# A fused two-layer diffusion step on one core: the last layer's gate modulation moved from the attention output projection into the feed-forward's input half

## The chip, the cores and the metric

One Trainium2 chip, one of its cores. The metric is the device time of one execution in microseconds (us). A core has TensorE (PE, matmuls; PEld are its weight loads), VectorE (DVE), ScalarE (ACT), GpSimd (POOL) and SyncE (SP, which issues most DMA transfers), each with its own instruction queue; they meet only through semaphores.

## The reference

Two trunk layers over 512 latent tokens and 128 context tokens (640 columns in all), width 1024. Each layer is a mixer (attention) and a SwiGLU feed-forward of inner width 2816, each with its own shift, scale and gate, that come from the conditions `c` and `c_ctx`. Cut to what matters here:

```
def ada_modulation(cond, w_mod, b_mod):
    m = jax.nn.silu(cond) @ w_mod + b_mod
    return jnp.split(m, 6, axis=-1)          # sh1, sc1, g1, sh2, sc2, g2

x = x + g1 * mixer_out                       # output projection of the mixer
h = modulate(rms_norm(x, norm_ffn[l]), sh2, sc2)
x = x + g2 * ((silu(gate) * up) @ w_ffn_out) # gate, up = split(h @ w_ffn_in)
```

The change concerns the last of the six, `g2` of layer 1: 1024 values for each of the two conditions. They are first used where the feed-forward's output is added to `x`.

## The kernel before

Activations lie transposed, in 8 tiles of 128 features x 640 tokens (`T`), worked on in two halves of 320 columns (`HT`). Every f32 product is made of three fp32r products: both operands are split into a high part (a copy on ACT) and a low part (a subtraction on DVE), and `mm3` (L184) multiplies high x high, high x low and low x high. So each weight costs ACT and DVE time as well as PE time.

The layers run one after the other. Within a layer, what the change touches:

- **mixer_out** (L982) is the output projection. It runs over 8 output blocks n; for each it loads the weights (`unit`, L172), multiplies, adds gate x product to the residual x[n] (`residual`, L318, DVE) and adds the squares to a running norm sum (`Norm.add`, L204: a square on ACT, an addition on DVE, tile `oanacc` in layer 0 and `ocnacc` in layer 1). The last three blocks are held back in their second half, and while PE multiplies these, the first half's norm is finished (`Norm.rstd`, L214): a matmul with ones (`oanp`, `ocnp`), then Ln and Exp on ACT.
- **gates_beside** (L1882) is called from layer 1's mixer_out after each block. It loads two of the eight gate rows (`wmG`, 512 KB each) and multiplies those loaded before by the Silu of the two condition rows (`cb`, tile tag "ws" of the feed-forward's pool), a DVE product with an accumulated sum for each row and condition (`junkG`, L1890): 16 products. The two Silu run on ACT at n = 0.
- **ModS** (L256) normalises and modulates x for the feed-forward and forms sums of halves (`add_up`, L305). It needs 16 scratch halves. In layer 0 six of them lie in a wide tile with tag "cb", in layer 1 in three tiles with tag "sg".
- **ffn** (L1079), input half: 22 blocks of the hidden width. Blocks 0 and 1 use eight products per half (`eight`); blocks 2 to 21 are the loop at L1320, where seven products of half the width take the place of eight. In a block PE runs products named by their operands (11, D, E of the block before, N, 21, 22, C). DVE and ACT work in an order written out by hand: `Line` (L1098) makes each DVE instruction follow the one before it, and so for ACT. Weights of block fb + 1 are summed and split during block fb (`Weights`, L1188). The hidden tile of a block is `sg`, its other factor `up`.
- In layer 1 (`paired`) blocks 7 to 18 form six pairs. `split_pair` (L1288) handles the hidden tile of the block before in three stages per block, and turns a pair into seven kinds of tiles (B11, B21, B22, T1 to T4) that go out to DRAM. The first block of a pair has the light share (two low halves, one subtraction), the second the heavy one. A pair's first tile must stay until the second's block is done. `sg` has three buffers of its own in layer 1; in layer 0 it shares the three buffers of tag "t" (`tmp`, L101) with `up`.
- **mod_side** (L1623) is how layer 0's feed-forward computes other modulations beside its work: `start` loads both condition rows into a tile "cb" through SP, `step("load", fb)` issues a row's load in the block before, and `step("fb", fb, dve)` puts the two products (`junk`) into DVE's written order, after the split stage and before `up`. For blocks 5 to 21 of layer 0 it is one row a block. Layer 1 passes a function that does nothing (L1912).
- **ffn**, output half: nine or ten first blocks (`FIRST`) are multiplied whole, the residual is added; then, in layer 1, seven products (`PLAN`, L1499) over the kinds of tiles, fetched from DRAM by `fetch_kind` (L1417). The last three kinds (T4, T1, B22; 18 tiles) go into slots that the first half of the output frees (L1548).

The order of each engine's queue is set by a planner from priorities and dependencies, except where `after` or a `Line` fixes it. Tiles with one tag share its buffers in rotation: a new one waits for the last reader of the oldest.

Of the kernel before, what the change touches and what calls it, by code (L numbers as in the profile page):

```python
# [11 lines left out]
F32 = mybir.dt.float32  # L12
# [37 lines left out]
def body(ctx, tc, xT, vecs, crow, wm0, wm0g, wm1, wA, wNV, wNA, wMK, wMV, wOA, wGQ, wGK, wGV, wOC,  # L50
# [50 lines left out]
    def tmp(name):  # L101
        return tp.tile([P, T], F32, tag="t", bufs=3, name=name)
# [153 lines left out]
    class ModS:  # L256


        def __init__(self, name, x, gsl, ml, sh, pools):
            pool, keep_, paired = pools  # L260

            if paired:
                a = [keep_.tile([P, T], F32, tag="sg", bufs=3, name=f"{name}32a{i}") for i in range(3)]
            else:
                a = [keep_.tile([P, 2 * D], F32, tag="cb", bufs=1, name=name + "32a")]
            d = [pool.tile([P, 1024], F32, tag="wr", bufs=2, name=f"{name}32d{i}") for i in range(2)]
            d += [pool.tile([P, 1024], F32, tag="w4", bufs=2, name=f"{name}32e{i}") for i in range(2)]
            room = [t[:, j * HT:j * HT + HT] for t, n in zip(a + d, ((2, 2, 2) if paired else (6,)) + (3, 3, 3, 1)) for j in range(n)]
            self.left, self.right = room[:KT], room[KT:]
            self.name, self.x, self.gsl, self.ml, self.sh = name, x, gsl, ml, sh  # L270
            self.act = {}
            self.q = [[ring.tile([P, T], F32R, tag=("hh", "hl")[i], name=f"{name}q{k}{i}") for k in range(KT)] for i in range(2)]
            self.sums = {c: [pool.tile([P, T], F32R, tag="sums", bufs=16, name=f"{name}{c}{k}") for k in range(4)]
                         for c in "DCNE"}
# [704 lines left out]
                wh, wl = un(w0)  # L979
                proj(pss[u][c], wh[0], wh[1], hh, hl, [k], *HALF[c], first=first and j == 0, last=last and j == n - 1, w0=wl)  # L980

    def mixer_out(wsrc, os_, order, xin, ml, name, nxt, pre, beside=None):  # L982

        nrm = Norm(name + "n", D)
        oh, ol = [o[0] for o in os_], [o[1] for o in os_]
        x = []
        ks = [(k, k) for k in order]
        if True:
            def wunit(n):
                get = lazy(lambda: unit(wsrc[n], 1024, f"{name}w{n}", lo="g" if n % 2 else "v"))  # L990
                return lambda w0: (get(), w0)

            def evac(n, c, ps):
                if c == 0:
                    x.append(xin(n))
                residual(x[n], x[n], ps, ml, G1, n, c)
                nrm.add(x[n], c)

            def half(ps, un, c, ks, first=True, last=True):
                two_halves([ps], [un], ks, oh, ol, c, first=first, last=last)  # L1000

            held = []
            units = [wunit(n) for n in range(KT)]
            for n in range(KT):
                un = units[n]
                if n < 2:
                    ps = pair(f"{name}{n}")
                    for c in range(2):
                        half(ps, un, c, ks[:-1], last=False)
                    held.append((ps, un))  # L1010
                    if n == 1:
                        for i, (ps, un) in enumerate(held):
                            for c in range(2):
                                half(ps, un, c, ks[-1:], first=False)
                                evac(i, c, ps[c])
                        held = []
                elif n < 5:
                    ps = pair(f"{name}{n}")
                    for c in range(2):
                        half(ps, un, c, ks)  # L1020
                        evac(n, c, ps[c])
                else:
                    ps = pair(f"{name}{n}") if n < 7 else [bank(f"{name}{n}{c}") for c in range(2)]
                    half(ps, un, 0, ks)
                    evac(n, 0, ps[0])
                    held.append((n, ps, un))
                if beside is not None:
                    if 0 < n < KT - 1:
                        units[n + 1](0)
                    beside(n, nrm.last)  # L1030
            pre()
            for j in range(KT - 2):
                for n, ps, un in held:
                    half(ps, un, 1, ks[j:j + 1], first=j == 0, last=False)
                if j >= 1:
                    nxt(x, nrm, 0, (j - 1,))
            for i, (n, ps, un) in enumerate(held):
                half(ps, un, 1, ks[-2:], first=False)
                evac(n, 1, ps[1])
                nxt(x, nrm, 0, (5 + i,))  # L1040
        return x, lambda: nxt(x, nrm, 1, range(KT))

    def next_mod(name, gsl, ml, sh, sums=None):

        box = {}

        def nxt(x, nrm, c, ks):
            if 0 in ks:
                nrm.rstd(c)
                if c == 0:  # L1050
                    box["m"] = Mod(name, x, gsl, ml, sh) if sums is None else ModS(name, x, gsl, ml, sh, sums)
            for k in ks:
                box["m"].make(c, nrm.rs, k)
        return box, nxt
# [24 lines left out]
    def ffn(l, x, pend, hm, nxt, side, opened):  # L1079
# [204 lines left out]
            dve(V.tensor_tensor, out, a, b, ALU.subtract)  # L1284

        over = {}

        def split_pair(jb, sg, stage):  # L1288
            i, j = PAIR_OF[jb]
# [30 lines left out]
        for fb in range(FEW, FB):  # L1320
# [2 lines left out]
            n = Weights(fb + 1) if fb < FB - 1 else None  # L1323
            b5 = bank(f"fd{l}_{fb}")
            up = tmp(f"up{l}_{fb}")
            sg = fk.tile([P, T], F32, tag="sg", bufs=3, name=f"sg{l}_{fb}") if paired else tmp(f"sg{l}_{fb}")
            both = paired and job and job[0] in PAIR_OF
            p5, u1, g2 = [utile(f"{c}{l}_{fb}") for c in ("p5", "u1", "g2")]
            if n:
# [68 lines left out]
        dve(V.tensor_tensor, jsg, jup, jsg, ALU.mult)  # L1398
        hidden(jb, jsg)
        fs.close()  # L1400

        fo = ph.enter_context(tc.tile_pool(name=f"fo{l}", bufs=1, reuse_waits="tile"))

# [5 lines left out]
        for i, fb in enumerate(FIRST[STAY:]):  # L1409
            if i < 6:  # L1410
                again(fb, [ring.tile([P, T], F32R, tag="hh" if i < 4 else "hl", name=f"hr{l}_{fb}{c}") for c in "hl"])
            else:
                again(fb, [fo.tile([P, T], F32R, tag="hd", bufs=26, name=f"hr{l}_{fb}{c}") for c in "hl"])
        later = [(c, i) for c in ("T2", "B11", "T3", "B21") for i in range(len(PAIRS))] if paired else list(SECOND)
        kinds = {}

        def fetch_kind(c, i, pool, tag):  # L1417
# [4 lines left out]
        def some(n):  # L1422
            for _ in range(min(2 * n if paired else n, len(later))):
                fb = later.pop(0)
                if paired:
                    fetch_kind(*fb, fo, "hd")
                    continue
                again(fb, [fo.tile([P, T], F32R, tag="hd", bufs=2 * len(SECOND), name=f"hr{l}_{fb}{c}") for c in "hl"])
# [48 lines left out]
        for i, (n, j0, m) in enumerate(jobs):  # L1477
# [5 lines left out]
            if j0 + m == len(FIRST):  # L1483
# [3 lines left out]
                    some(2)  # L1487
                step("n", n)
        some(len(later))

        exp_tables(last)
        nrm = Norm(f"fn{l}", D)
# [5 lines left out]
        if paired:  # L1498
# [48 lines left out]
                weights(j)  # L1547
            spots = [("hl", 4), ("hh", 8), ("hl", 4), ("fo", 2)]  # L1548
            spots = [c for c, n in spots for _ in range(n)]
            for c, i in [(c, i) for c in ("T4", "T1", "B22") for i in range(len(PAIRS))]:  # L1550
                tag = spots.pop(0)
                fetch_kind(c, i, *((fo, "hd") if tag == "fo" else (ring, tag)))
            for p in range(4):
# [112 lines left out]
        return xk  # L1666

    op = ffn_open(0)
    box, nxt = next_mod("h01", gs[0][1], mods[0], SH2, (op[5], op[1], False))
    x, pend = mixer_out(wOA, oMs + oNs, [4, 5, 6, 7, 0, 1, 2, 3], x_again, mods[0], "oa", nxt, op[-1])  # L1670
    box2, nxt = next_mod("h10", gs[1][0], mods[1], SH1)
    side = mod_side([(0, wm0g, G2)] + [(1, wm1[j:j + 8], j) for j in (SH1, SC1, G1, SH2, SC2)],
# [200 lines left out]

    open_y(y=4)
    op = ffn_open(1)
    box, nxt = next_mod("h11", gs[1][1], mods[1], SH2, (op[5], op[1], True))
    cb = [op[5].tile([P, D], F32, tag="ws", bufs=2, name=f"cb{c}") for c in range(2)]
    for c in range(2):
        nc.scalar.dma_start(cb[c], bass.AP(tensor=crow.tensor, offset=crow.offset + D * c, ap=[[0, P], [1, D]]))
    gates = []  # L1880

    def gates_beside(n, done):  # L1882
        if n == 0:
            for c in range(2):
                S.activation(cb[c], cb[c], AF.Silu)
        while gates:
            i, raw = gates.pop(0)
            for c in range(2):
                junk = op[1].tile([P, D], mybir.dt.bfloat16, tag="junk", bufs=1, name=f"junkG{i}{c}")
                after(done, lambda: V.scalar_tensor_tensor(junk, raw, 1.0, cb[c], ALU.mult, ALU.mult,  # L1890
                                                           accum_out=mods[1][:, G2 + i, c:c + 1]))
        if n < 4:
            for i in (2 * n, 2 * n + 1):
                raw = op[5].tile([P, D], F32, tag="wr", bufs=2, name=f"wmG{i}")
                nc.sync.dma_start(raw, wm1[G2 + i])
                gates.append((i, raw))
        elif n == 4:
            m = mods[1][:, G2:G2 + 8, :]
            V.tensor_tensor(m, m, bc2(bmod(1, G2, 8)), ALU.add)

    x, pend = mixer_out(wOC, oGs, list(range(8)), lambda n, x=x: x[n], mods[1], "oc", nxt, op[-1], gates_beside)

    def final(x, nrm, c, ks):
        c0, c1 = HALF[c]
# [4 lines left out]
            (nc.sync if k % 2 else nc.scalar).dma_start(yT[:, k, c0:c1], x[k][:, c0:c1])  # L1909
        return last  # L1910

    x, pend = ffn(1, x, pend, box["m"], final, lambda fk: lambda *a: None, op)  # L1912
    pend()


# [154 lines left out]
```

## Time and profile before

| what | value |
|---|---|
| median of 3 runs | 1523.57 us (1522.32 to 1525.17) |
| profiled execution | 1523.39 us, its span 1521.6 us |
| PE, DVE, ACT, POOL busy | 1459.4, 1192.5, 767.3, 223.5 us |
| moved by DMA | 226.89 MB, mean 149 GB/s |
| layer 1's 16 gate products (junkG), 1039 to 1074 us | 23.5 us of DVE |
| one block of the input half, either layer | 12.34 us |

How to read it: busy times are of one execution, in us. A group of instructions is shown as line, engine, operation, output<-input, shapes, count | busy us, mean ns | idle time before it and who ended it. In an order of time, the first two columns are start and duration in us, and "[0.67 <-PE fd L62]" is the time that the engine sat idle before the instruction and what released it. In the view of windows the columns are: length in us, then busy time and number of instructions of PE, PEld, DVE, ACT and POOL, the granted TensorE clock (1.00 is full), the busy share of the DMA engines and GB/s. The names of layer 0 begin with oa, h01; those of layer 1 with oc, h11; fg, fu, fd are banks of the feed-forward's input half, fo those of its output half.

### The profile page before, as it was taken

The numbers are of one execution on the slowest core, as the hardware profiler recorded it, in microseconds if no ns is written. First come the engines' busy times: TensorE is split into PE (matmuls) and PEld (weight loads), VectorE is DVE, ScalarE is ACT, GpSimd is POOL, SyncE is SP. The second block draws the span as 40 slices with busy tenths as digits, with TensorE's granted clock in tenths as the row PEclk, the third lists the DMA queues.
The fourth block names the chain that finished last, engine by engine and source line by source line (L and its number), as shares of the span: only waits on it lengthen the run. The fifth ranks groups of instructions, "written<-read, shape, count | busy, mean of one in ns | idle before, by whom it ended". The sixth has DMA issues, their size and how long they took to land.

```text
span 1521.6 us, 25799 instructions
## 1 busy us (share of the span) xinstructions
PE 1459.4 (96%) x9856; PEld 1404.0 (92%) x9856; DVE 1192.5 (78%) x2234; ACT 767.3 (50%) x1506; POOL 223.5 (15%) x295
## 2 busy tenths in 40 slices
PE   5999989989999999999999999999899999999996
PEld 4888878879999999999999889989899999999996
DVE  5646687885899999967998787778898889854486
ACT  5535586773755444441124556663665555542242
POOL 0225544522000000000002433222000000000000
PEclk9999999999999999999999999999999999999998
DMA  9324540005155555569763210014235445458531
GB/s 371 115 94 152 186 143 34 29 15 181 55 177 177 179 184 188 176 228 342 258 213 114 91 42 29 29 66 143 98 136 163 161 161 192 163 200 312 189 112 69
DMA packets 79579, 226.89 MB, mean 149 GB/s; under 512 B 8816, under 2 KB 14208, under 8 KB 79328
## 3 DMA queue, kind: packets, MB, share of 16 engines
q1 hardware_dynamic: 77120, 220.84, 42.8%
q10 hardware_dynamic: 1920, 3.47, 0.7%
q8 instruction: 77, 1.26, 0.3%
q0 software_dynamic: 416, 0.93, 0.2%
q14 instruction: 46, 0.38, 0.1%
HBM read 190.86 MB, written 34.36 MB: 148 GB/s over the span
## 4 chain that ended last, share of the span: by engine, by line
PE 77%; DVE 13%; ACT 4%; DMA 4%; issue 2%; POOL 0%; DVEq 0%; SPq 0%; ACTq 0%; POOLq 0%
PE fg L62 19%; PE fd L62 9%; PE fo L62 7%; PE fu L62 5%; PE gq L62 2%; PE nk L62 2%; PE fo_2b L62 1%; PE nq L62 1%; PE go L62 1%; DVE junkG L1890 1%; DMA mraw<-in_wm 1%; PE fo_2a L62 1%; PE ms L62 1%; PE gs L62 1%; PE mod L62 1%
## 5 line engine op out<-in xcount | busy, mean ns | idle before, releaser
L1104 ACT ACTIVATE sg<-g 128x320 f32<-128x320 f32 x40 | 18.9, 472 | 132.2 <-DVE g L1104 132.2
L1638 DVE SCALAR_TENSOR_TENSOR junk<-wm,cb 128x1024 bf16<-128x1024 f32 x62 | 75.7, 1221 | 6.4 <-DMA wm<-in_wm 5.7
L62 PE MATMUL gq<-h10h,wgq 128*128 128x320 f32 x256 | 66.4, 319 | 0.4 <-DVE gb L1821 0.3
L251 POOL TENSOR_SCALAR h10h<-h10t,gs,mods 128x320 fp32r<-128x320 f32 x4 | 3.5, 887 | 429.4 <-DVE h10t L245 427.7
L1104 DVE TENSOR_TENSOR wY<-s,wY 128x1024 fp32r<-128x1024 f32 x40 | 48.8, 1220 | 1.1 <-ACT wY L1104 1.1
L1104 DVE TENSOR_TENSOR wZ<-s,wZ 128x1024 fp32r<-128x1024 f32 x40 | 48.8, 1219 | 0.0
L62 PEld LDWEIGHTS gq<-h10h,wgq 128*128 128x128 f32 x256 | 45.3, 190 | 1.6 <-PE gtp L66 0.8
L1104 ACT ACTIVATE wZ<-s 128x1024 fp32r<-128x1024 f32 x40 | 42.4, 1060 | 1.1 <-DVE s L1104 1.0
L1104 ACT ACTIVATE wY<-s 128x1024 fp32r<-128x1024 f32 x40 | 42.0, 1049 | 0.0
L1104 DVE SCALAR_TENSOR_TENSOR junk<-wm,cb 128x1024 bf16<-128x1024 f32 x34 | 41.5, 1220 | 0.6
L1822 ACT ACTIVATE gp<-gs,gb,rq 128x640 f32<-128x640 f32 (+1 forms) x40 | 31.9, 797 | 19.5 <-DVE gb L1821 15.4
L1104 DVE TENSOR_TENSOR sg<-up,sg 128x640 f32<-128x640 f32 (+1 forms) x40 | 31.4, 786 | 12.2 <-ACT sg L1104 12.2
L62 PE MATMUL gq<-h10l,wgq 128*128 128x320 f32 x128 | 39.8, 311 | 0.0
L62 PE MATMUL fg<-h11E,wW 128*128 128x320 f32 x240 | 38.7, 310 | 0.4 <-DVE g L1104 0.4
L62 PE MATMUL fd<-h11q,wZ 128*128 128x320 f32 x240 | 38.6, 310 | 0.2 <-ACT p L1104 0.2
L62 PE MATMUL fg<-h11N,wZ 128*128 128x320 f32 x240 | 38.7, 309 | 0.0
L62 PE MATMUL fg<-h11q,wX 128*128 128x320 f32 x240 | 38.6, 309 | 0.0
L62 PE MATMUL fg<-h01q,wX 128*128 128x320 f32 x240 | 38.6, 309 | 0.0
L62 PE MATMUL fg<-h01N,wZ 128*128 128x320 f32 x240 | 38.6, 309 | 0.0
L62 PE MATMUL fu<-h11q,wX 128*128 128x320 f32 x240 | 38.6, 309 | 0.0
L62 PE MATMUL fu<-h01q,wX 128*128 128x320 f32 x240 | 38.6, 309 | 0.0
L62 PE MATMUL fg<-h01E,wW 128*128 128x320 f32 x240 | 38.6, 310 | 0.0
(3187 smaller groups left out, 5295.3 us busy)
## 6 DMA issues: line engine op xcount, KB each, us to landing
wm<-in_wm SPq DMA_DIRECT2D x40, 512.0 KB, 4.0
mraw<-in_wm SPq DMA_DIRECT2D x24, 512.0 KB, 3.6
mraw<-in_wm SPq DMA_DIRECT2D x8, 1024.0 KB, 15.3
hr_T<-sp_T SPq DMA_DIRECT2D x24, 320.0 KB, 6.1
hr_B<-sp_B SPq DMA_DIRECT2D x18, 320.0 KB, 6.7
wm<-in_wm0g SPq DMA_DIRECT2D x8, 512.0 KB, 3.4
wmG<-in_wm SPq DMA_DIRECT2D x8, 512.0 KB, 4.2
x<-in_xT SPq DMA_DIRECT2D x8, 320.0 KB, 5.4
```

The lines of the kernel that those rows point to most:

```text
L62: cls.last = nc.tensor.matmul(*a, **k)
L251: G.tensor_scalar(h[:, c0:c1], t, self.gsl[:, k, 0:1], self.ml[:, self.sh + k, 0:1], ALU.mult, ALU.add)
L1104: self.last = after(self.last, lambda: op(*a, **k))
L1638: def step(kind, at, line=lambda op, *a, **k: op(*a, **k)):
L1822: S.activation(dst, src, AF.Exp, bias=nb, scale=rq[:, j:j + 1], accum_out=ll[:, j:j + 1])
L1890: after(done, lambda: V.scalar_tensor_tensor(junk, raw, 1.0, cb[c], ALU.mult, ALU.mult, accum_out=mods[1][:, G2 + i, c:c + 1]))
```

## The change

gates_beside, its condition rows and its call go, and so does mixer_out's hook for it. Layer 1's feed-forward gets a mod_side of its own: one gate row in each of blocks 5, 6, 8, 10, 12, 14, 16 and 18. That needs the tile "cb" (8 KB of each partition) in a pool that had the three "sg" tiles, so these go: a pair's first hidden tile is `lead`, a ninth tile of the residual's tag and so in the place of x[0]. x[0] is written to DRAM before the loop and read back into `lead` after it. All other `sg` of layer 1 are `tmp` tiles, as in layer 0. ModS uses the "cb" tile for its scratch halves in both layers. After the gates, the "cb" tile holds three of the six T4 tiles (`more`), fetched ahead of the other kinds.

```diff
         def __init__(self, name, x, gsl, ml, sh, pools):
-            pool, keep_, paired = pools
-            if paired:
-                a = [keep_.tile([P, T], F32, tag="sg", bufs=3, name=f"{name}32a{i}") for i in range(3)]
-            else:
-                a = [keep_.tile([P, 2 * D], F32, tag="cb", bufs=1, name=name + "32a")]
+            pool, keep_ = pools
+            a = keep_.tile([P, 2 * D], F32, tag="cb", bufs=1, name=name + "32a")
...
-    def mixer_out(wsrc, os_, order, xin, ml, name, nxt, pre, beside=None):
+    def mixer_out(wsrc, os_, order, xin, ml, name, nxt, pre):
...
-                if beside is not None:
-                    if 0 < n < KT - 1:
-                        units[n + 1](0)
-                    beside(n, nrm.last)
...
         over = {}
+        if paired:
+            x0 = dr.tile([P, T], F32, name=f"x0_{l}")
+            nc.sync.dma_start(x0, x[0])
+            lead = ring.tile([P, T], F32, tag="x", name=f"lead{l}")
...
-            sg = fk.tile([P, T], F32, tag="sg", bufs=3, name=f"sg{l}_{fb}") if paired else tmp(f"sg{l}_{fb}")
+            sg = lead if paired and PAIR_OF.get(fb, (0, 1))[1] == 0 else tmp(f"sg{l}_{fb}")
...
         fs.close()
+        if paired:
+            nc.sync.dma_start(lead, x0)
+            x = [lead] + x[1:]
...
+        if paired:
+            wide_ = fk.tile([P, 2 * D], F32R, tag="cb", bufs=1, name=f"more{l}")
+            more = [wide_[:, j * T:(j + 1) * T] for j in range(3)]
...
         some(len(later))
+        if paired:
+            for i, t in enumerate(more):
+                nc.sync.dma_start(f(t), solo["T4", i])
+                kinds["T4", i] = t
...
-            for c, i in [(c, i) for c in ("T4", "T1", "B22") for i in range(len(PAIRS))]:
+            for c, i in [(c, i) for c in ("T4", "T1", "B22") for i in range(len(PAIRS))][len(more):]:
...
-    box, nxt = next_mod("h11", gs[1][1], mods[1], SH2, (op[5], op[1], True))
-    cb = [op[5].tile([P, D], F32, tag="ws", bufs=2, name=f"cb{c}") for c in range(2)]
-    for c in range(2):
-        nc.scalar.dma_start(cb[c], bass.AP(tensor=crow.tensor, offset=crow.offset + D * c, ap=[[0, P], [1, D]]))
-    gates = []
-    def gates_beside(n, done):
...
-    x, pend = mixer_out(wOC, oGs, list(range(8)), lambda n, x=x: x[n], mods[1], "oc", nxt, op[-1], gates_beside)
+    box, nxt = next_mod("h11", gs[1][1], mods[1], SH2, (op[5], op[1]))
+    x, pend = mixer_out(wOC, oGs, list(range(8)), lambda n, x=x: x[n], mods[1], "oc", nxt, op[-1])
...
-    x, pend = ffn(1, x, pend, box["m"], final, lambda fk: lambda *a: None, op)
+    side = mod_side([(1, wm1[G2:], G2)], lambda kind, i: int(kind == "fb" and i in (5, 6, 8, 10, 12, 14, 16, 18)))
+    x, pend = ffn(1, x, pend, box["m"], final, side, op)
```

More of the change, by code (lines that the diff above doesn't have):

```diff
@@ L259, in __init__ @@
         def __init__(self, name, x, gsl, ml, sh, pools):
-            pool, keep_, paired = pools
-            if paired:
-                a = [keep_.tile([P, T], F32, tag="sg", bufs=3, name=f"{name}32a{i}") for i in range(3)]
-            else:
-                a = [keep_.tile([P, 2 * D], F32, tag="cb", bufs=1, name=name + "32a")]
+            pool, keep_ = pools
+            a = keep_.tile([P, 2 * D], F32, tag="cb", bufs=1, name=name + "32a")
             d = [pool.tile([P, 1024], F32, tag="wr", bufs=2, name=f"{name}32d{i}") for i in range(2)]
             d += [pool.tile([P, 1024], F32, tag="w4", bufs=2, name=f"{name}32e{i}") for i in range(2)]
-            room = [t[:, j * HT:j * HT + HT] for t, n in zip(a + d, ((2, 2, 2) if paired else (6,)) + (3, 3, 3, 1)) for j in range(n)]
+            room = [t[:, j * HT:j * HT + HT] for t, n in zip([a] + d, (6, 3, 3, 3, 1)) for j in range(n)]
             self.left, self.right = room[:KT], room[KT:]
@@ L1668, in body @@
     op = ffn_open(0)
-    box, nxt = next_mod("h01", gs[0][1], mods[0], SH2, (op[5], op[1], False))
+    box, nxt = next_mod("h01", gs[0][1], mods[0], SH2, (op[5], op[1]))
     x, pend = mixer_out(wOA, oMs + oNs, [4, 5, 6, 7, 0, 1, 2, 3], x_again, mods[0], "oa", nxt, op[-1])
@@ L1875, in body @@
     op = ffn_open(1)
-    box, nxt = next_mod("h11", gs[1][1], mods[1], SH2, (op[5], op[1], True))
-    cb = [op[5].tile([P, D], F32, tag="ws", bufs=2, name=f"cb{c}") for c in range(2)]
-    for c in range(2):
-        nc.scalar.dma_start(cb[c], bass.AP(tensor=crow.tensor, offset=crow.offset + D * c, ap=[[0, P], [1, D]]))
-    gates = []
-    def gates_beside(n, done):
[L1883 to L1899, printed above, removed]
-    x, pend = mixer_out(wOC, oGs, list(range(8)), lambda n, x=x: x[n], mods[1], "oc", nxt, op[-1], gates_beside)
+    box, nxt = next_mod("h11", gs[1][1], mods[1], SH2, (op[5], op[1]))
+    x, pend = mixer_out(wOC, oGs, list(range(8)), lambda n, x=x: x[n], mods[1], "oc", nxt, op[-1])
     def final(x, nrm, c, ks):
```

## The prediction, made before the changed kernel ran

> **What bounds the kernel now.** I read the page first: TensorE (PE) is busy 96% of the span, and the chain that ended last is mostly PE lines. Of what the change moves, one VectorE (DVE) line shows in it, junkG, with 1%, about 15 us.
>
> ```profile
> span 1521.6 us, 25799 instructions
> ...
> PE 1459.4 (96%) x9856; PEld 1404.0 (92%) x9856; DVE 1192.5 (78%) x2234; ACT 767.3 (50%) x1506; POOL 223.5 (15%) x295
> ...
> PE fg L62 19%; PE fd L62 9%; PE fo L62 7%; PE fu L62 5%; PE gq L62 2%; PE nk L62 2%; PE fo_2b L62 1%; PE nq L62 1%; PE go L62 1%; DVE junkG L1890 1%; DMA mraw<-in_wm 1%; PE fo_2a L62 1%; PE ms L62 1%; PE gs L62 1%; PE mod L62 1%
> ```
>
> So a saving counts only where PE waits. The waits of PE, next, show two that this change can touch: the layer 1 norm sum (ocnp) waits 6.2 us for DVE, and one product of the feed-forward's output half (fo_1b) waits 0.8 us for a weight copy. Layer 0's norm sum (oanp), computed by the same function without gates beside it, waits 0.6.
>
> ```profile
> PE ocnp L62 <- DVE ocnacc L211: 6.2, 2, 6.0
> ...
> PE fo_1b L62 <- ACT wo_1S L1534: 0.8, 1, 0.8
> PE oanp L62 <- DVE oanacc L211: 0.6, 1, 0.6
> ```
>
> The kernel holds its own control experiment. Layer 0 runs mixer_out, ModS and ffn with no gates in the projection and with its modulation in the feed-forward's input half, as layer 1 will. I compare the two from the chain in order of time (start, us, what), between marks that both have: the second projection product and the first fg product of the loop's second block.
>
> ```profile
> 342.57 3.08 PE oa0b L62 x21
> ...
> 447.13 3.52 PE fg L62 x24
> ...
> 1023.85 3.08 PE oc0b L62 x21
> ...
> 1137.61 3.52 PE fg L62 x24
> ```
>
> The windows between these marks (us; busy time and instructions of PE, PEld, DVE, ACT, POOL; granted clock; DMA) hold the same 705 matmuls:
>
> ```profile
> 342.57:447.13 104.56, 103.96 (x705) 103.27 (x705) 78.38 (x152) 54.33 (x104) 13.32 (x8) 1.00 0.40 135
> 1023.85:1137.61 113.76, 106.64 (x705) 104.67 (x705) 96.14 (x177) 62.33 (x111) 13.64 (x8) 0.97 0.38 129
> ...
> 1076.60:1080.10 3.50, 3.49 (x11) 3.10 (x12) 0.00 (x0) 2.19 (x4) 0.00 (x0) 0.50 0.78 272
> ```
>
> Layer 1 takes 113.76 - 104.56 = 9.20 us longer. Of that, 113.76 - 106.64 = 7.12 against 0.60 is idle PE (6.5 us more), and 106.64 - 103.96 = 2.7 us is slower PE: after the long wait the granted clock stands at 0.50 for 3.5 us.
>
> **Part 1: the gates leave the projection.** Removed there are 16 products on DVE and their accumulator reads, eight 512 KB loads on SP, two Silu on ACT and two loads of the condition rows.
>
> ```profile
> L1890 DVE SCALAR_TENSOR_TENSOR junkG<-wmG,cb 128x1024 bf16<-128x1024 f32 x16 | 23.5, 1471 | 0.1
> ...
> 1078.08 0.53 ACT L218 ACTIVATE ocnrs<-ocnp,eps 128x320 f32<-128x320 f32 x1 [1.28 <-PE ocnp L62]
> 1078.63 1.28 ACT L219 ACT_TABLE_LOAD   x1
> 1079.92 0.47 ACT L219 ACTIVATE ocnrs<-ocnrs 128x320 f32<-128x320 f32 x1
> ...
> L218 ACT ACT_TABLE_LOAD x2 | 2.6, 1283 | 0.0
> L219 ACT ACT_TABLE_LOAD x2 | 2.6, 1283 | 0.0
> ```
>
> 23.5 us of DVE goes, where DVE sits in front of the residuals and norm sums on which ocnp waits. The early Silu also replaced the table that holds Ln and Exp together: each half's rstd then reloads twice, 4 x 1.28 us, and the Silu itself once. What is late next without them is what layer 0 shows: its ocnp twin waits 0.6 us, nothing else in that stretch of PE waits visibly. So the stage gives 9.20 us. Ends: all of PE's idle gone would be 9.8; if only the wait of 6.2 went and the rest stayed behind another cause, 6.2. I take 9.20, since it is a measured difference over equal work.
>
> At most three of the four stand on a chain (after the first, Ln still waits 1.28 us for PE): 3 x 1.28 = 3.8 us, part of the 9.20 and not beside it. The Trainium skill (ScalarE: Activation LUTs, section What ACT_TABLE_LOAD costs) puts a switch at 1.28 us for the load and 1.38 for a drain, 2.66 together; by that these would be 8.0 us, and the part of the stage that they could explain 4.2 us larger. The trace does not show the drain here: Ln ends at 1078.61, the load starts at 1078.63, and Exp starts 0.01 us after it.
>
> **Part 2: the gates enter the input half.** PE is busy without a gap there in both layers, 12.33 to 12.34 us a block (rows below), so the added work is free as long as DVE keeps up. Price of a pair of products, from layer 0's loop: from 544.42 to the next operation at 546.83, 2.41 us; eight pairs are 19.3 us. They go to blocks 5, 6, 8, 10, ... 18: where pairs are split, only to the even blocks, which carry the light share of the split. The DVE column of four windows of a block each, cut at DVE's own block start (odd, even), and a layer 0 block with its gate pair:
>
> ```profile
> 1225.96:1238.29 12.33, 12.33 (x86) 12.33 (x85) 11.94 (x21) 7.46 (x14) 0.00 (x0) 1.00 0.43 150
> 1238.29:1250.63 12.34, 12.34 (x86) 12.34 (x85) 10.20 (x16) 6.27 (x11) 0.00 (x0) 1.00 0.62 209
> ...
> 533.48:545.81 12.33, 12.33 (x86) 12.33 (x85) 11.99 (x20) 6.06 (x10) 0.00 (x0) 1.00 0.58 188
> ...
> L1104 DVE SCALAR_TENSOR_TENSOR junk<-wm,cb 128x1024 bf16<-128x1024 f32 x34 | 41.5, 1220 | 0.6
> ...
> 544.42 1.22 DVE L1104 SCALAR_TENSOR_TENSOR junk<-wm,cb 128x1024 bf16<-128x1024 f32 x1
> ...
> 546.83 0.48 DVE L1104 TENSOR_TENSOR up<-fd,u 128x320 f32<-128x320 f32 x1
> ```
>
> An even block becomes 10.20 + 2.41 = 12.61, over the 12.33; with the odd one, 12.61 + 11.94 = 24.55 of 24.67. It fits by 0.12. Place by place: in an even block the last split half ends near 1247.8, and DVE then idles 0.67 and 1.26 us. The row of PE is that of the next block's E product.
>
> ```profile
> 1247.37 0.49 DVE L1104 TENSOR_TENSOR hd_2l<-sg,hd_2l 128x320 fp32r<-128x320 f32 x1
> 1248.54 0.49 DVE L1104 TENSOR_TENSOR up<-fd,u 128x320 f32<-128x320 f32 x1 [0.67 <-PE fd L62]
> 1250.29 0.49 DVE L1104 TENSOR_TENSOR g<-fg,p 128x320 f32<-128x320 f32 x1 [1.26 <-PE fg L62]
> ...
> 1253.62 1.92 PE L62 MATMUL fg<-h11E,wW 128*128 128x320 f32 x12
> ...
> 1262.61 0.49 DVE L1104 TENSOR_TENSOR g<-fg,p 128x320 f32<-128x320 f32 x1 [0.29 <-PE fg L62]
> ```
>
> The gate pair runs 1247.8 to 1250.2, up follows to 1250.6, and g starts 0.3 us late. Behind the gate on DVE stand up, g and the next block's weight sums; behind g, ACT's Silu. PE needs g's bank again at 1253.62 for the E product, 1253.62 - 1250.78 = 2.8 us after g has read it now, so 0.3 is covered; the odd block's own 0.29 of idle gives it back. Weight halves have more room: those of a block are written in the block before. Cost taken: nothing; ends: 0 and the whole 19.3 if DVE's idle could not be filled. I stay at zero: layer 0 does it at 11.99 of 12.33 without a wait of PE.
>
> **Part 3: SP, spill and buffers.** Three transfers of 320 KB are new in kind: x[0] out before the loop, back after it, and the lead tile waits for the first at the end of block 7. A 320 KB load takes 5.4 us, and block 7 comes some 60 us later. On the way back the reload waits for the last split's reads, at 1335.8; queued behind it on SP is the first hidden block, which leaves only at 1349.23 now; x[0] is used at 1377.95. Cover 13 and 42 us, cost zero; with that cover gone it would be the transfer, 5.4. The second halves of pairs take the shared temporaries, as every block of layer 0 does, so I charge nothing. The condition rows now load through SP, where they wait for ModS's room, with spills queued behind: in layer 0 the first of these leaves at 429.75, 17.4 us before the mark 447.13, in layer 1 now at 1121.53, 16.1 before 1137.61, so nothing is later for it.
>
> ```profile
> x<-in_xT SPq DMA_DIRECT2D x8, 320.0 KB, 5.4
> ...
> 1335.32 0.48 DVE L1104 TENSOR_TENSOR hd_0l<-sg,hd_0l 128x320 fp32r<-128x320 f32 x1
> ...
> 1349.23 0.32 SPq L1406 DMA_DIRECT2D hr_0h<-sp_0h  x1
> ...
> 1377.95 0.55 DVE L322 SCALAR_TENSOR_TENSOR xr<-fo_0a,mods,xr 128x320 f32<-128x320 f32 x1 [0.64 <-PE fo_0a L62]
> ...
> 429.75 0.33 SPq L1138 DMA_DIRECT2D sp_0h<-hd_0h  x1
> ...
> 1121.53 0.33 SPq L1138 DMA_DIRECT2D sp_0h<-hd_0h  x1
> ```
>
> **Part 4: three T4 tiles early.** The old gate-row tile takes them before the rest. Today all of these loads fill SP when the first output half ends:
>
> ```profile
> 1428.20 7.83 SPq L1419 DMA_DIRECT2D hr_T<-sp_T  x12
> 1436.53 4.97 SPq L1419 DMA_DIRECT2D hr_B<-sp_B  x6
> 1442.65 0.33 SPq L1506 DMA_DIRECT2D wo_3A22r<-in_wFO  x1
> ```
>
> 18 loads take 1442.65 - 1428.20 = 14.45 us, 0.80 each; three fewer bring the weight behind them 2.4 us forward, and PE waited 0.83 for what is made of it. Gain 0.83; ends 0 (they collide with other weights) and 0.83.
>
> **The sum.** The profiled execution took 1523.39 us (span 1521.6); the median is 0.18 above. 1523.39 - 9.20 - 0.83 = 1513.36; against the median, 1513.5.
>
> **Rivals.** (1) DVE becomes the bound. The Trainium skill (Perfetto Trace Analysis, Identifying the Most-Contended Engine) calls VectorE's occupancy a fair measure of how near it is to its limit and would have the most contended engine improved. The mechanism by rows: 24.55 of 24.67 is 99.5%; if the idle places of DVE are not where the gates come, they lengthen the eight blocks by 2.41 each, 19.3 less the 2.8 that the bank's lead hides once, and the end is 1513.5 + 16.5 = 1530.0: slower. It turns from gain to loss when a pair of blocks is over by (10.0 + 2.8) / 6 = 2.1 us, a product of 2.3 us instead of 1.22. Against it: POOL, beside which junkG averaged 1.47 us, is idle in this half, and layer 0's 34 products average 1.22. Layer 0 does not bear the rule out at 97%; 99.5% no run shows yet. Chance 0.04. (2) Something other than the gates holds layer 1's norm sum, and only the 6.2 of the wait returns, or DVE's lag costs PE a few us: 1523.57 - 6.2 - 0.83 = 1516.5, up to 1520. Against it: equal matmuls and the same code in layer 0. Chance 0.16. (3) The freed time comes back as another wait altogether (a spill, the reload of x[0]), within 0.2%: 0.03. That T4's early loads go out no earlier costs 0.83, 1514.3, inside the forecast, which has 0.77.
>
> **Numbers.** About 0.2%, 3 us, can be told from no change. Faster by more: 0.77 + 0.16 = 0.93; same 0.03; slower 0.04. The low end is the 9.8 and 0.83 off the median, 1512.9, less 1.2 for the spread of the runs below it (1522.32), 1511.7; the high end is rival 2 with as much more, 1517.7.
>
> **What would show it.** Right: no wait of ocnp above 1 us, granted clock 1.00 throughout the projection, two table loads fewer per rstd, the marks 104.6 us apart, blocks still 12.34 us with DVE near 12.6 and 11.9, no fo_1b wait. Wrong: PE waiting for DVE or ACT inside the loop, blocks longer where gates are, or products well over 1.22 us.

## The result, and the profile after

The changed kernel takes 1512.2 us (median of 6 runs, 1509.52 to 1518.67) against 1523.53 (6 runs, 1521.34 to 1525.17): a ratio of 0.9931 with a 95% interval of 0.9911 to 0.9951, so 7.5 to 13.6 us faster. By the medians it is 11.3 us; the forecast was 1513.5, or 10.0 us. The profiled execution took 1513.06 us; the sum, made against the profiled time, had said 1513.36. That the two lie 0.3 us apart is in part luck, since executions of the changed kernel spread over 9 us; the stages below are the better test.

The page of the kernel after: span, busy times, and the chain that ended last by engine and by line. No line of the gates is left in it, and PE's share of the chain has grown to 84%.

```profile
span 1511.3 us, 25796 instructions
...
PE 1455.6 (96%) x9856; PEld 1401.0 (93%) x9856; DVE 1191.1 (79%) x2234; ACT 760.1 (50%) x1501; POOL 224.6 (15%) x295
...
PE 84%; DVE 8%; ACT 4%; DMA 2%; issue 2%; POOL 0%; DVEq 0%; SPq 0%; ACTq 0%; POOLq 0%
PE fg L62 20%; PE fd L62 9%; PE fo L62 7%; PE fu L62 6%; PE gq L62 2%; PE nq L62 2%; PE nk L62 2%; PE fo_2b L62 1%; PE fo_0b L62 1%; DMA mraw<-in_wm 1%; PE go L62 1%; PE fo_2a L62 1%; PE fo_0a L62 1%; PE mod L62 1%; PE ms L62 1%
```

The waits of PE, after. The two layers' norm sums now wait alike, and fo_1b, which stood between them in the list before, waits no more:

```profile
PE ocnp L62 <- DVE ocnacc L211: 0.6, 1, 0.6
PE oanp L62 <- DVE oanacc L211: 0.6, 1, 0.6
```

The windows, after: layer 1 between the two marks of the prediction, then the rest of the program cut at the loop's end and at three places of the output half (the columns are those of the prediction's windows).

```profile
1023.89:1128.45 104.56, 103.96 (x706) 103.27 (x705) 77.85 (x144) 53.84 (x104) 13.60 (x8) 1.00 0.30 103
...
1128.45:1343.14 214.69, 214.69 (x1467) 214.61 (x1466) 204.34 (x317) 117.99 (x209) 0.00 (x0) 1.00 0.56 189
1343.14:1415.38 72.24, 72.24 (x495) 72.13 (x494) 27.24 (x46) 16.94 (x26) 0.00 (x0) 1.00 0.71 245
1415.38:1461.10 45.72, 45.72 (x314) 45.72 (x314) 34.08 (x57) 18.33 (x29) 0.00 (x0) 1.00 0.52 182
```

The same cuts in the kernel before:

```profile
1137.61:1352.30 214.69, 214.69 (x1466) 214.62 (x1466) 186.70 (x284) 116.59 (x207) 0.00 (x0) 1.00 0.49 163
1352.30:1424.54 72.24, 72.24 (x494) 72.13 (x494) 27.70 (x47) 17.31 (x27) 0.00 (x0) 1.00 0.71 245
1424.54:1470.26 45.72, 44.89 (x306) 44.63 (x306) 33.21 (x53) 17.54 (x27) 0.00 (x0) 1.00 0.57 199
```

The reader sees where the time went. Between the marks, 113.76 us became 104.56, with the same matmuls and full clock. In the loop, DVE rose from 186.7 to 204.3 us and PE did not notice: 214.69 us both times. In the output half's middle, PE gets through 314 matmuls in 45.72 us instead of 306. Nothing was given back elsewhere.

### The profile page after: what moved, and what is told of

Read it like the earlier page. It is cut to its first block, busy times and chain, and to the rows that moved or that the text cites. A ratio compares the mean times of both kernels' runs of the same rounds, so it can differ in the third digit from the quotient of the medians.

```text
span 1511.3 us, 25796 instructions
## 1 busy us (share of the span) xinstructions
PE 1455.6 (96%) x9856; PEld 1401.0 (93%) x9856; DVE 1191.1 (79%) x2234; ACT 760.1 (50%) x1501; POOL 224.6 (15%) x295
## 3 DMA queue, kind: packets, MB, share of 16 engines
q8 instruction: 77, 1.26, 0.3%
## 4 chain that ended last, share of the span: by engine, by line
PE 84%; DVE 8%; ACT 4%; DMA 2%; issue 2%; POOL 0%; DVEq 0%; SPq 0%; ACTq 0%; POOLq 0%
PE fg L62 20%; PE fd L62 9%; PE fo L62 7%; PE fu L62 6%; PE gq L62 2%; PE nq L62 2%; PE nk L62 2%; PE fo_2b L62 1%; PE fo_0b L62 1%; DMA mraw<-in_wm 1%; PE go L62 1%; PE fo_2a L62 1%; PE fo_0a L62 1%; PE mod L62 1%; PE ms L62 1%
## 5 line engine op out<-in xcount | busy, mean ns | idle before, releaser
L1645 DVE SCALAR_TENSOR_TENSOR junk<-wm,cb 128x1024 bf16<-128x1024 f32 x62 | 75.6, 1219 | 7.1 <-DMA wm<-in_wm 6.6
L1097 DVE SCALAR_TENSOR_TENSOR junk<-wm,cb 128x1024 bf16<-128x1024 f32 x50 | 61.0, 1220 | 0.8
L62 PE MATMUL fd<-h01q,wZ 128*128 128x320 f32 x240 | 38.5, 309 | 0.0
L62 PE MATMUL fg<-h11C,wY 128*128 128x320 f32 x240 | 38.5, 309 | 0.0
```

Source lines behind the costliest of these rows:

```text
L62: cls.last = nc.tensor.matmul(*a, **k)
L1097: self.last = after(self.last, lambda: op(*a, **k))
L1645: def step(kind, at, line=lambda op, *a, **k: op(*a, **k)):
```

## The experiments

Times are medians, and each ratio is against runs of the kernel before that were taken beside them. For the stages I use the marks of the trace. Between the two marks, the changed kernel took 104.56 us and the five kernels below that leave this stage as it is 104.57 to 105.1, so differences under 0.6 us there say nothing.

**Which part of the projection cost what.** Two cuts of the kernel before, each alone and both together.

```diff
-                S.activation(cb[c], cb[c], AF.Silu)
+                S.activation(cb[c], cb[c], AF.Copy)
```

> The kernel before, with the Silu of the two condition rows in the projection replaced by a plain copy (the gates then come from the conditions without Silu); no table is switched there, and the 16 products stay. Theory (the products on VectorE hold the norm sum): the wait of ocnp stays near 6 us, the stretch between the marks falls from 113.76 by 0 to 1.5 us, so 1522 to 1523.5 us. Rival (the table loads on the chain are the price): the stretch falls by about 3.8 us or more, to 1519.7 us or less.

Measured: 1521.48 us, ratio 1.0000 (0.9991 to 1.0009). The wait stayed, and the stretch fell by 0.81 us to 112.95:

```profile
PE ocnp L62 <- DVE ocnacc L211: 5.9, 1, 5.9
...
1021.70:1134.65 112.95, 106.72 (x705) 105.30 (x705) 96.87 (x177) 55.84 (x106) 13.87 (x8) 0.97 0.39 130
```

```diff
-                after(done, lambda: V.scalar_tensor_tensor(junk, raw, 1.0, cb[c], ALU.mult, ALU.mult,
-                                                           accum_out=mods[1][:, G2 + i, c:c + 1]))
+                after(done, lambda: V.tensor_tensor(mods[1][:, G2 + i, c:c + 1], raw[:, :1], cb[c][:, :1], ALU.mult))
```

> The kernel before, with each of the 16 gate products cut to one column (the gates are then not the sums); loads, Silu and table switches stay. Theory: 23.5 us of VectorE go, the wait of ocnp falls below 1 us plus at most one table load, the clock stays at 1.00, the stretch falls by 7.5 to 9.2 us to 104.6 to 106.3, the time to 1514.3 to 1516 us. Rival (table loads): the stretch falls by 5.4 us or less, the time stays above 1518 us.

Measured: 1516.3 us, ratio 0.9965 (0.9954 to 0.9977). The wait of ocnp falls from 6.2 to 1.6 us and the clock is full, but the stretch, cut at 705 matmuls, is 106.96: down by 6.80, not by 7.5 to 9.2. My number was missed on the low side; the rival's limit of 5.4 was passed. The first 45.32 us are as in layer 0 with 310 matmuls, and what is missing is missing behind them: 380 matmuls in 59.24 us, against 396 with both cuts.

```profile
PE ocnp L62 <- DVE ocnacc L211: 1.6, 2, 1.3
...
1026.29:1071.61 45.32, 45.32 (x310) 45.06 (x308) 26.04 (x51) 17.32 (x26) 9.70 (x4) 1.00 0.57 198
1071.61:1130.85 59.24, 56.72 (x380) 55.77 (x380) 53.63 (x110) 43.44 (x82) 3.00 (x4) 1.00 0.29 93
...
1026.29:1133.25 106.96, 104.44 (x705) 103.22 (x704) 80.27 (x161) 62.53 (x110) 12.70 (x8) 1.00 0.40 137
```

Both edits together:

> The kernel before with both cuts: one-column products and a copy for the Silu (gates not computed as the reference does); only the loads stay. Both theories: the stretch is 104.6 us, as in layer 0, and the time 1523.5 - 9.2 = 1514.3 us; the fo_1b wait of 0.8 us stays. If the loads on SyncE had a part in it, the stretch stays above 105.5 us.

Measured: 1513.9 us, ratio 0.9948 (0.9933 to 0.9963), stretch 104.58. The row loads on SP and the hook that orders the weight loads, which both stay in this kernel, had no part in it.

```profile
1024.18:1069.50 45.32, 45.32 (x310) 45.32 (x310) 25.08 (x51) 15.80 (x24) 9.72 (x4) 1.00 0.62 209
1069.50:1128.74 59.24, 58.64 (x396) 57.95 (x395) 54.06 (x110) 40.15 (x82) 3.00 (x4) 1.00 0.27 88
...
1024.18:1128.76 104.58, 103.98 (x705) 103.29 (x705) 79.14 (x161) 55.97 (x106) 12.73 (x8) 1.00 0.42 140
```

So of 9.18 us, the products are worth 6.80 if they go first and 8.37 if they go last, and the Silu with its table switches 2.38 if it goes last but only 0.81 if it goes first. As long as the products delay the norm, most of the reloading hides behind that delay. The 0.81 is hardly above the scatter of the marks, and the run times cannot tell it from nothing; the other three prices stand clear of that scatter.

**What the gates cost where they are now.** The products in layer 1's input half, cut to one column:

```diff
+                        if len(todo) == 1:
+                            line(V.tensor_tensor, mods[l][:, j0 + i, c:c + 1], raw[:, :1], cb[:, c, :1], ALU.mult)
+                            continue
                         junk = fp.tile([P, D], mybir.dt.bfloat16, tag="junk", ...)
```

> The changed kernel, with the 16 products in layer 1's input half cut to one column (gates not the sums); rows are still loaded. Theory (VectorE fills idle time there): VectorE falls by about 18 us, the loop's blocks stay at 12.34 us, the time is the changed kernel's within 0.3 us. Rival (VectorE at 99.5% costs PE a little): 1 to 3 us faster than the changed kernel.

Measured: 1511.34 us, ratio 0.9939 (0.9923 to 0.9956), which is the changed kernel's within the intervals; and the loop is exactly as long, while DVE fell by 16.4 us.

```profile
1125.98:1340.67 214.69, 214.69 (x1467) 214.61 (x1466) 187.95 (x301) 118.18 (x209) 0.00 (x0) 1.00 0.56 189
```

**Where free ends.** Each product made twice, so four in a gate block:

```diff
+                      for again in range(1 + (len(todo) == 1)):
...
                         line(V.scalar_tensor_tensor, junk, raw, 1.0, cb[:, c, :], ALU.mult, ALU.mult, ...)
```

> The changed kernel, with each of the 16 products of layer 1's input half made twice (same result): 2.41 us more on VectorE in each gate block. A pair of blocks then needs 24.55 + 2.41 = 26.96 us of VectorE against 24.67. Theory (VectorE runs behind until g is 2.8 us late and then holds PE at the E product): loss of 1.3 us in block 6, 0.9 in block 8, 2.3 in each of 10 to 18: 13.6 us, so about 1526 us, with PE waiting for VectorE's g before the product with wW. Rival A (full price): 19.3 us, 1531.5 us. Rival B (only the weights' lead of 8 us counts): 8.4 us, 1520.6 us.

Measured: 1529.63 us, ratio 1.0049 (1.0032 to 1.0067), 17.4 us above the changed kernel's median. The loop alone, cut at the same marks, takes 231.53 us, 16.84 more. The place is the one expected: PE waits seven times, each time before the product with wW and for g. The size is not; it lies between the theory's 13.6 and the full price of 19.3. The sum of the waits, and five of the seven E products in PE's order of time (what lies between them is left out):

```profile
PE fg L62 <- DVE g L1097: 9.8, 7, 2.1
...
1177.16 2.02 PE L62 MATMUL fg<-h11E,wW 128*128 128x320 f32 x12 [1.26 <-DVE g L1097]
...
1202.82 2.02 PE L62 MATMUL fg<-h11E,wW 128*128 128x320 f32 x12 [0.65 <-DVE g L1097]
...
1229.88 3.38 PE L62 MATMUL fg<-h11E,wW 128*128 128x320 f32 x12 [2.12 <-DVE g L1097]
...
1284.15 3.10 PE L62 MATMUL fg<-h11E,wW 128*128 128x320 f32 x12 [2.12 <-DVE g L1097]
...
1338.51 2.88 PE L62 MATMUL fg<-h11E,wW 128*128 128x320 f32 x12 [2.10 <-DVE g L1097]
```

From 1229.88 to 1284.15 lie two pairs, 27.13 us each and not 26.96: DVE is busy in 53.34 of these 54.27 us, and short gaps between its instructions make up the rest. That is 0.17 a pair more than forecast, 1.0 in all. And wherever the wait was 2.1 us, the 12 matmuls behind it took 2.9 to 3.4 us instead of 2.0. The windows of the same kernel around one such wait, granted clock before the last two columns:

```profile
1227.76:1229.88 2.12, 0.00 (x1) 0.00 (x0) 2.09 (x5) 0.02 (x1) 0.00 (x0) 1.00 0.00 0
1229.88:1231.40 1.52, 1.51 (x6) 1.52 (x7) 1.49 (x3) 1.52 (x3) 0.00 (x0) 0.58 0.90 218
1231.40:1233.07 1.67, 1.67 (x9) 1.67 (x7) 1.64 (x3) 1.67 (x3) 0.00 (x0) 0.50 0.32 125
```

In the middle of the loop PE has to wait for DVE anyhow, so a slow stretch there only takes the place of waiting. The last one comes in the last gate block, and nothing makes up for it: E and the product after it take 5.17 us instead of the 3.64 behind the wait at 1311.35, so 1.5 us are lost. Whether the room before E is really 2.8 us, this run alone leaves open. A run with half the overload, three products in a gate block, helps to tell:

```diff
+                      for again in range(1 + (len(todo) == 1 and c == 0)):
```

> The changed kernel, with one of the two products of a gate block made twice (three products, same result): 1.26 us more in each gate block, half the overload of the run with four. A pair then needs about 25.9 us of VectorE against 24.67. Theory (the room before the E product is used up first, then each pair is held by what it is over): blocks 5 and 6 run 1.7 us behind, block 7 takes that back, blocks 8 and 10 use up the 2.8 us, and 12 to 18 lose about 1.2 each: 4.8 us in the loop, the waits of PE under 1.5 us and the granted clock at 1.00 all through. Rival A (there is no room, every pair loses all of it, as the run with four seemed to): 7 us or more. Rival B (the loss of the run with four was its clock): under 3 us.

Measured: 1516.25 us, ratio 0.9963 (0.9950 to 0.9975). The loop's 1466 matmuls take 219.63 us instead of 214.69, so 4.9 us, as the theory said; the waits are four, in the last four gate blocks, none above 0.93 us, at full clock.

```profile
PE fg L62 <- DVE g L1097: 3.1, 4, 0.9
...
1126.87:1346.50 219.63, 216.50 (x1466) 214.66 (x1466) 212.63 (x333) 115.98 (x209) 0.00 (x0) 1.00 0.57 187
```

Rivals A and B are out: the room exists, is used up first, and from then on each pair loses about what it is over. But the agreement on 4.8 us is in part luck, as the order of time shows. In the gate blocks where PE waits, in this run and in the run with four, PE's queue has the 12 matmuls of fu ahead of E, where the changed kernel goes from D straight to E. The last gate block, of the changed kernel and then of the run with three:

```profile
1316.60 1.92 PE L62 MATMUL fd<-h11D,wY 128*128 128x320 f32 x12
1318.35 1.92 PE L62 MATMUL fg<-h11E,wW 128*128 128x320 f32 x12
```

```profile
1320.46 1.92 PE L62 MATMUL fu<-h11q,wX 128*128 128x320 f32 x12
1323.31 2.03 PE L62 MATMUL fg<-h11E,wW 128*128 128x320 f32 x12 [0.93 <-DVE g L1097]
```

So PE has about 1.76 us more to do before it needs g (12 matmuls of 214.69 / 1466 us), and the room is 2.83 + 1.76 = 4.59 us instead of 2.8. On the other side DVE falls further behind than the theory had it: block 7 does not take all of the delay back, its g is still 1.82 us late. The last gate block's g in the kernel before, in the run with three and in the run with four:

```profile
1324.17 0.49 DVE L1104 TENSOR_TENSOR g<-fg,p 128x320 f32<-128x320 f32 x1 [1.26 <-PE fg L62]
```

```profile
1322.77 0.48 DVE L1097 TENSOR_TENSOR g<-fg,p 128x320 f32<-128x320 f32 x1
```

```profile
1337.97 0.48 DVE L1097 TENSOR_TENSOR g<-fg,p 128x320 f32<-128x320 f32 x1
```

Counted from each kernel's second mark, g comes 9.34 us later with three products and 19.77 us later with four. Less the room of 4.59 this gives 4.75 us, of 4.94 measured, and 15.18 us, which with the 1.5 us of the last slow stretch is 16.7 of the 16.84 measured. That accounts for both runs to within 0.2 us: the price is DVE's delay at the last gate block, less the room, plus the clock. The theory had two terms wrong, room and delay, by about 1.8 us each, and with three products they cancelled.

**Does the place between the light sums matter?** The gates in the heavy blocks:

```diff
-int(kind == "fb" and i in (5, 6, 8, 10, 12, 14, 16, 18))
+int(kind == "fb" and i in (5, 6, 9, 11, 13, 15, 17, 19))
```

> The changed kernel, with the six gates of the pairs in the blocks with the heavy share of the split (9, 11, ... 19) instead of the light ones. VectorE needs 11.94 + 2.41 = 14.35 us in such a block and 10.20 in the next; the sum of a pair is the same. Theory (2.8 us of room before the E product): g is up to 2.1 us late, PE does not wait, same time as the changed kernel within 0.3 us. Rival (the place between the light sums is what makes it free): each of six blocks is about 2 us longer, 12 us in all.

Measured: 1512.24 us, ratio 0.9931 (0.9915 to 0.9948). The same as the change. In a heavy block, g now ends at 1253.32 + 0.48 = 1253.80 and E begins at 1254.59 without a wait; 0.8 us of the room is left (0.7 to 0.8 in all six blocks).

```profile
1253.32 0.48 DVE L1097 TENSOR_TENSOR g<-fg,p 128x320 f32<-128x320 f32 x1
...
1254.59 1.63 PE L62 MATMUL fg<-h11E,wW 128*128 128x320 f32 x10
```

So the light blocks are the safer place, and for the time they make no difference.

**The early T4 tiles**, undone alone:

```diff
-            more = [wide_[:, j * T:(j + 1) * T] for j in range(3)]
+            more = []
```

> The changed kernel without the early fetch of three T4 tiles (all 18 tiles of the last three kinds are fetched when the first output half ends). Theory: the weight behind them leaves about 2.4 us later, the fo_1b wait of 0.8 us is back, time 0.8 to 1.1 us above the changed kernel. Rival (the wait went for another reason): no wait, same time.

Measured: 1514.68 us, ratio 0.9942 (0.9927 to 0.9957). The medians are 2.5 us apart, with intervals that overlap, and from the second mark to the end the profile is 1.94 us longer than the changed kernel's: the direction is the one expected, the size about twice. The trace shows the mechanism. The wait is back, and SP sends the weight 14.3 us after the first of 18 tiles:

```profile
PE fo_1b L62 <- ACT wo_1S L1541: 1.2, 1, 1.2
...
1419.15 7.71 SPq L1422 DMA_DIRECT2D hr_T<-sp_T  x12
...
1433.41 0.33 SPq L1513 DMA_DIRECT2D wo_3A22r<-in_wFO  x1
```

In the changed kernel, SP's queue at the same place sends it 10.5 us after the first of 15:

```profile
1419.50 5.22 SPq L1422 DMA_DIRECT2D hr_T<-sp_T  x9
...
1429.96 0.33 SPq L1513 DMA_DIRECT2D wo_3A22r<-in_wFO  x1
```

All five kernels that fetch 18 tiles at this place have the wait, of 0.5 to 1.4 us in their profiles, and the five that fetch 15 have none. The spill of x[0] was not priced by itself. No run pointed to a version faster than the change.

## Why the prediction was right

**Part 1, the projection.** The measured difference between the layers, 9.20 us, came back: 104.57 and 104.56 us in the two layers of the profiled execution, up to 105.1 in later ones. ACT loads a table 6 times instead of 11, so the four loads of the norms and the Silu's own are gone, and ocnp waits 0.6 us. Comparing with a stage of the same code that lacked the work was the strongest step. The weak sentence in it was the account of the tables, "at most three of the four stand on a chain: 3.8 us". As an upper bound it holds, but the worth depends on what stands beside it, 0.81 or 2.38 us. The Trainium skill (ScalarE: Activation LUTs, What ACT_TABLE_LOAD costs) gives 2.66 us for a switch with its drain; by that three switches would be 8.0 us. These runs do not bear out a drain on the chain: removing the switches last gave 2.38 us, less than two loads of 1.28.

**Part 2, the input half.** No cost, as forecast. DVE's columns in an odd and an even block, cut as in the prediction, are 12.22 and 12.10 where 11.94 and 12.61 were expected: DVE works past the block's end and into the next, and the sum, 24.32 of 24.67, is 0.23 lower than forecast. The gate pair itself is busy for 2.38 of its 2.41 us; but where DVE has no idle time left, neighbours overlap (below, up takes 0.49 us and g starts 0.40 after it), and the overlap counts once. Place by place it went as worked out. In the order of time, the gates take the idle time behind hd_2l, and g of the even block starts at 1241.45. Before, at the same phase, it was 1250.29, 9.16 us later by the marks, which makes it 0.3 us late; the odd block's g is late by 0.02. A product takes 1.22 us here. In the projection the mean had been 1.47, but that is no general price: 14 of the 16 took 1.21 to 1.23 us, and the two that started while POOL ran a tensor operation (1043.06 for 2.96 us, 1060.92 for 2.66 us) took 3.10 and 3.43. In the loop POOL is idle.

```profile
1216.80:1229.13 12.33, 12.33 (x86) 12.33 (x86) 12.22 (x22) 7.46 (x14) 0.00 (x0) 1.00 0.55 179
1229.13:1241.47 12.34, 12.34 (x86) 12.34 (x85) 12.10 (x20) 6.21 (x11) 0.00 (x0) 1.00 0.61 225
```

```profile
1238.23 0.49 DVE L1097 TENSOR_TENSOR hd_2l<-lead,hd_2l 128x320 fp32r<-128x320 f32 x1
1238.64 1.22 DVE L1097 SCALAR_TENSOR_TENSOR junk<-wm,cb 128x1024 bf16<-128x1024 f32 x1
...
1241.05 0.49 DVE L1097 TENSOR_TENSOR up<-fd,u 128x320 f32<-128x320 f32 x1
1241.45 0.48 DVE L1097 TENSOR_TENSOR g<-fg,p 128x320 f32<-128x320 f32 x1
...
1253.47 0.49 DVE L1097 TENSOR_TENSOR g<-fg,p 128x320 f32<-128x320 f32 x1
```

**Part 3, spill and queues.** The reload of x[0] leaves on SP 12.5 us ahead of the first hidden block, and x[0] is first used at 1368.82, 41 us after it: covers of 13 and 42 us had been forecast.

```profile
1327.64 0.66 SPq L1399 DMA_DIRECT2D lead<-x  x1
...
1340.10 0.32 SPq L1406 DMA_DIRECT2D hr_0h<-sp_0h  x1
...
1368.82 0.55 DVE L319 SCALAR_TENSOR_TENSOR lead<-fo_0a,mods,lead 128x320 f32<-128x320 f32 x1 [0.65 <-PE fo_0a L62]
```

**Part 4, T4.** The 0.83 us of PE's wait went, and the stretch around it moved by 8 matmuls, about 1.2 us at 0.15 us each; where the other 0.3 us come from stays open. The mechanism was right; that the size fits so well is luck, since the same wait was 0.5 to 1.4 us in other kernels that have it. From the second mark to the end, the gain is (1521.6 - 1137.61) - (1511.3 - 1128.45) = 1.14 us; this and the 9.2 are the whole difference of the profiled executions, but for the start, 0.04.

**The rival that DVE becomes the bound** was rightly unlikely, and the runs with three and four products show that its mechanism is real. Its point of reversal was set too high: "a product of 2.3 us instead of 1.22", where twice the work (2.44 us) already costs 17 us, more than the 10 gained. The formula, six pairs of 2.29 us less a room of 2.8, would have given 10.9. It left out the delay that stays from blocks 5 and 6, DVE's gaps and the clock, 1.5 us; and its room of 2.8 us, read where PE goes from D to E, was 4.6 once PE's queue had fu ahead.

## What to carry to other kernels

Where a program runs the same stage twice, once with and once without a piece of work, cut both by equal counts of matmuls: the difference is the price of the piece with everything that hangs on it, and it held here within 0.6 us where a sum of instructions would have said 23.5. Work that is put on an engine in strict order is free as long as the engine's sum stays under the period and the one result that the bound engine takes from it has room; both can be read from the trace beforehand, 24.55 of 24.67 us and 2.8 us here. The room holds for one order of the bound engine's queue: in the two overloaded kernels that order was another and the room 4.6 us, so a theory that hits the total should also be tested term by term. Two costs that hide behind each other must be taken out in both orders before either is given a size.

## What the runs showed of the hardware that was not expected

Three waits of PE of only 2.10 to 2.12 us, in the run with four products, were each followed by about 3.4 us at half the granted clock (0.58, 0.66 and 0.71 in the windows right behind the waits, then 0.50). The waits of 0.65 to 1.26 us in that loop were not, and neither was a wait of 1.99 us in layer 0 of the same run (before PE's product at 227.15, with the clock at 1.00 from there to 235.00). Whether the length alone decides, these runs do not show. The Trainium skill (TensorE: Matmul & The Clock Gate, HAM oscillation — how this bites in real kernels) gives the rule that PE's idle gaps should stay under about 3.4 us. By that these waits would have been harmless; the measured rows decide that shorter ones can be enough.

The spread between executions of one kernel, 9 us for the changed one, seems to arise at least in part long before the changed stage. The same product of layer 0 starts in the chain of two kernels, which share their code up to there, 4.7 us apart (products cut to one column in the loop, then each made twice):

```profile
340.80 3.08 PE oa0b L62 x21
```

```profile
345.53 3.08 PE oa0b L62 x21
```

Up to that product PE runs 2095 matmuls in both, and is busy for 308.4 and 310.8 us; from 120 to 180 and from 300 to 341 us the granted clock is 1.00 in the first and 0.97 and 0.96 in the second. So about half of the 4.7 us is a slower PE and the rest is waiting. What brings it about stays open.
